# A decoder layer with PEER experts: second search over 96 candidate sums, index gather in fp16

## The chip, the cores and the metric

The kernel runs on one core of a Trainium2 chip. The metric is device time in microseconds, from several timed runs of the same program; beside them there is one profiled execution, from which all the rows below come. The engines are called TensorE (PE; PEld is its weight load), VectorE (DVE), ScalarE (ACT), GpSimd (POOL) and SyncE (SP, which issues the DMAs).

## The reference, cut to what matters

The layer mixes tokens with two attention groups and then runs a PEER block on 256 tokens. Only the PEER block is touched. For each token and each of 8 heads it takes the best 16 of two lists of 128 scores, forms all 256 sums of the two, takes the best 16 sums, and looks up which experts they stand for:

```python
v1, i1 = lax.top_k(s1, P_TOPK)            # P_TOPK = 16, s1 and s2 are (T, 8, 128)
v2, i2 = lax.top_k(s2, P_TOPK)
cand = (v1[..., :, None] + v2[..., None, :]).reshape(T, P_HEADS, P_TOPK * P_TOPK)
vals, ci = lax.top_k(cand, P_TOPK)
e = (jnp.take_along_axis(i1, ci // P_TOPK, axis=-1) * N_KEYS
     + jnp.take_along_axis(i2, ci % P_TOPK, axis=-1))
g = jax.nn.softmax(vals, axis=-1)
...
a = jnp.einsum('cd,ckd->ck', xc, expert_u[ec])
w = (gc * jax.nn.gelu(a.astype(jnp.float32))).astype(x.dtype)
return jnp.einsum('ck,ckd->cd', w, expert_v[ec])
```

Both lists come out in descending order, so a sum of the a-th of one and the b-th of the other (from 0) is beaten or equalled by (a+1)(b+1) - 1 others; only pairs with (a+1)(b+1) up to 16 can be among the best 16.

## The kernel before

The kernel does not gather experts. It computes all 128 x 128 experts densely: for each of 128 rows of `u` a product with the tokens (`xproj`, 24 matmuls, line 1101, output `a`), a GELU, a product with a routing weight per token and expert, and then a product with each row of `v` (line 1456, output `y`). The routing weights are built from the 16 chosen pairs of each head by one-hot matrices (`onehots`, lines 1287 and 1291, fp16) multiplied on TensorE (`route_mm`, line 1299, output `g`), four tokens at a time, 64 groups in all. `route_out` (lines 1312 and 1314) brings a group to its place.

The front part (attention, the query projection with `wq`) ends at some 221 us; then a step of the loop over `u` follows for each j from 0 to 127 (s = 16 + j in the code), and at 636 us the loop over `v` begins. Each 512 KB row is loaded by SyncE five steps ahead into one of three `raw` buffers (`load`, line 754). Three steps ahead it is split into two parts of lower precision (`split`): `hi` by ScalarE (line 769), then `lo` = raw - hi, 1024 columns, by VectorE or by GpSimd (line 772). `xproj` of step j first uses `hi` (16 matmuls), then `lo` (8 matmuls). The load of j+3 waits for `lo` of j, which frees its buffer.

Which engine makes `lo` is decided when `split` is called: GpSimd while `state["single"]` is True, otherwise VectorE. `single` is True during the two searches of `topk_steps`.

The order of all instructions is written out by hand (`manual_schedule`): each engine works through its instructions in the order in which the code emits them. VectorE's side work is a generator, `work_steps`, and each step calls `work_for(share)`, which adds `share` to a credit (at most 4.0) and takes pieces of work as long as the credit is positive. Each piece gives its own price in a `yield`; `yield None` ends the step's turn. In the loop over `u` the share is 3.15, less 1.3 if this step's `lo` is VectorE's.

For each half of the tokens (tt = 0, 1: 128 tokens each) the side work is:

- first search (lines 1212 to 1217): for 16 score lists of 128, find the best 8, their places, strike them out, and find the next 8;
- line 1220: the places converted to fp32; line 1225: the 256 sums of each head, in two instructions of 1024 elements;
- second search (lines 1231 to 1236): the same over 256 sums for each of 8 heads;
- lines 1241 to 1246: the softmax's argument, and the place split into its two indices by a shift and a mask;
- lines 1254, 1257, 1259: for each of the two indices, in two pieces of 64: compare with 0 to 15, multiply with the places found first, sum up over 16 (a gather by one-hot);
- lines 1265 to 1268: the softmax's end; then `topk_out`: transposes on TensorE (line 1274), and copies of the results into `idx` and `gf` (lines 1279 to 1281).

After both halves the routing starts: each piece is one group of `route_out`, `onehots` and `route_mm` and costs 1.95. In steps j=2 and j=4 `sums` puts a few small VectorE operations (lines 1360 to 1365) and a power on GpSimd (line 151) between the searches.

Of the kernel before, what the change touches and what calls it, by code (L numbers as in the profile page):

```python
# [30 lines left out]
C_I16 = 128  # L31
# [55 lines left out]
def body(tc, nc, ap, dbg=None):  # L87
    V, A, T, G, S = nc.vector, nc.scalar, nc.tensor, nc.gpsimd, nc.sync
# [6 lines left out]
    with ExitStack() as ctx:  # L95
# [74 lines left out]
        con = cst.tile([128, C_N], F32, name="con")  # L170
# [569 lines left out]
        raws, parts, pend, on_vector = {}, {}, {}, {}  # L740
# [37 lines left out]
        h = x  # L778
# [393 lines left out]
        cand = tk[:, 0:2048].rearrange("p (h a b) -> p h a b", h=8, a=16)  # L1172
        candf = tk[:, 0:2048].rearrange("p (h n) -> p h n", h=8)
        top = tk[:, 2048:2304].rearrange("p (m k) -> p m k", m=16)
        ixf = tk[:, 2304:2560].rearrange("p (m k) -> p m k", m=16)
        vals = tk[:, 2560:2688].rearrange("p (h k) -> p h k", h=8)
        res = tk[:, 2688:3072].rearrange("p (a m) -> p a m", a=3)
        abf = tk[:, 3072:3328].rearrange("p (a m) -> p a m", a=2)
        ixu = tk[:, 3328:3584].bitcast(U32).rearrange("p (m k) -> p m k", m=16)
        ciu = tk[:, 3584:3712].bitcast(U32).rearrange("p (h k) -> p h k", h=8)  # L1180
        abu = tk[:, 3712:3968].bitcast(U32).rearrange("p (a m) -> p a m", a=2)
        eq = sqq[:, 0:1024]
        rq = cst.tile([128, 16], F32, name="rq")
        iot = misc[:, 48:112].bitcast(F16)

# [19 lines left out]
        def topk_steps(tt):  # L1205
            state["single"] = True
            for m in range(16):
                while m >= state["scores"]:
                    yield None
                v8 = top[:, m, :]  # L1210
                s = sc[:, tt, m, :]
# [7 lines left out]
            state["single"] = False  # L1219
            V.tensor_copy(ixf, ixu)  # L1220
            yield 0.3
            tv = top.rearrange("p (h two) k -> p h two k", two=2)
            for q in range(2):
                hs_ = slice(q * 4, q * 4 + 4)
                V.tensor_tensor(cand[:, hs_], tv[:, hs_, 0, :, None].broadcast_to((128, 4, 16, 16)), tv[:, hs_, 1, None, :].broadcast_to((128, 4, 16, 16)), op=ALU.add)
                yield 1.25
            state["single"] = True
            for h in range(8):
                v8 = vals[:, h, :]
                s = candf[:, h, :]  # L1230
                V.max(out=v8[:, 0:8], in_=s)
                V.max_index(out=ciu[:, h, 0:8], in_max=v8[:, 0:8], in_values=s)  # L1232
                V.match_replace(out=s, in_to_replace=v8[:, 0:8], in_values=s, imm_value=LOWEST)  # L1233
                yield 1.45
                V.max(out=v8[:, 8:16], in_=s)
                V.max_index(out=ciu[:, h, 8:16], in_max=v8[:, 8:16], in_values=s)  # L1236
                yield 0.95
            state["single"] = False

            g = res[:, 2, :].rearrange("p (h k) -> p h k", h=8)  # L1240
            V.tensor_tensor(g, vals, vals[:, :, 0:1].broadcast_to((128, 8, 16)), op=ALU.subtract)
            V.tensor_tensor(g, g, rq[:, tt * 8:(tt + 1) * 8, None].broadcast_to((128, 8, 16)), op=ALU.mult)
            cf = ciu.rearrange("p h k -> p (h k)")
            V.tensor_scalar(abu[:, 0, :], cf, 4, None, op0=ALU.logical_shift_right)
            V.tensor_scalar(abu[:, 1, :], cf, 15, None, op0=ALU.bitwise_and)
            V.tensor_copy(abf, abu)
            yield 1.4
            iv = ixf.rearrange("p (h two) k -> p h two k", two=2)
            i16 = con[:, C_I16:C_I16 + 16]
            for w in range(2):  # L1250
                for q in range(2):
                    e4 = eq.rearrange("p (h k a) -> p h k a", h=4, k=16)
                    e3 = eq.rearrange("p (m a) -> p m a", m=64)
                    V.tensor_tensor(e3, i16[:, None, :].broadcast_to((128, 64, 16)),  # L1254
                                    abf[:, w, q * 64:(q + 1) * 64, None].broadcast_to((128, 64, 16)), op=ALU.is_equal)
                    yield 1.25
                    V.tensor_tensor(e4, e4, iv[:, q * 4:(q + 1) * 4, w, None, :].broadcast_to((128, 4, 16, 16)), op=ALU.mult)
                    yield 1.25
                    V.tensor_reduce(out=res[:, w, q * 64:(q + 1) * 64], in_=e3, axis=AX.X, op=ALU.add)
                    yield 1.25  # L1260
                if w == 0:

                    A.activation(out=g, in_=g, func=AF.Exp)
# [138 lines left out]
        for s in range(NQ, NQ + NU):  # L1402
# [28 lines left out]
                    (G if j < 127 else V).tensor_tensor(dst[:, :, :td], a[:, :, :td], dst[:, :, :td], op=ALU.mult)  # L1431
                state["done"] = j + 1
            td = state["routed"]
            work_for(3.15 - (1.3 if on_vector.get(s + 3) else 0))


        ya = [[bank("y") for n in range(2)] for tt in range(2)]
# [94 lines left out]
```

## Time and profile before

| | |
|---|---|
| median of 3 timed runs | 987.67 us (987.41 to 989.28) |
| profiled execution, its own time | 989.98 us |
| its span, first to last instruction | 988.2 us |
| mean granted TensorE clock | 0.981 of full speed |
| TensorE matmul busy | 949.2 us (96%) |
| VectorE busy | 742.2 us (75%) |
| ScalarE busy | 499.1 us (51%) |
| GpSimd busy | 184.9 us (19%) |

A busy time is the sum of an engine's instructions in the span. A timeline names each instruction with its start, its duration, its engine, line, operation and tiles, and in brackets the idle time before it with what ended it. Durations of neighbours on VectorE overlap by some 0.08 us, so that what an instruction costs in a row of its kind is the distance of the starts.

### The profile page before, as it was taken

The numbers are of one execution on the slowest core, as the hardware profiler recorded it, in microseconds if no ns is written. First come the engines' busy times: TensorE is split into PE (matmuls) and PEld (weight loads), VectorE is DVE, ScalarE is ACT, GpSimd is POOL, SyncE is SP. The second block draws the span as 40 slices with busy tenths as digits, with TensorE's granted clock in tenths as the row PEclk, the third lists the DMA queues.
The fourth block names the chain that finished last, engine by engine and source line by source line (L and its number), as shares of the span: only waits on it lengthen the run. The fifth ranks groups of instructions, "written<-read, shape, count | busy, mean of one in ns | idle before, by whom it ended". The sixth has DMA issues, their size and how long they took to land.

```text
span 988.2 us, 17195 instructions
## 1 busy us (share of the span) xinstructions
PE 949.2 (96%) x6657; PEld 858.0 (87%) x6657; DVE 742.2 (75%) x1379; ACT 499.1 (51%) x920; POOL 184.9 (19%) x148
## 2 busy tenths in 40 slices
PE   7699899999799898999999999999999999999998
PEld 6487678999799898999999999988888888888886
DVE  7576988777989997888999998566666666666664
ACT  4445766655264354555445444455554444455552
POOL 5462524265207500000011112100000000000000
PEclk9799999999799998999999999999999999999999
DMA  7522521654466456455545545565666565665664
GB/s 240 206 91 85 188 66 48 209 171 130 129 205 198 145 157 211 135 166 161 159 151 168 153 152 169 189 194 193 193 193 195 194 195 196 195 193 192 193 192 149
DMA packets 48958, 166.74 MB, mean 169 GB/s; under 512 B 7276, under 2 KB 8300, under 8 KB 48620
## 3 DMA queue, kind: packets, MB, share of 16 engines
q1 hardware_dynamic: 48876, 165.64, 52.9%
q8 instruction: 52, 0.85, 0.3%
q14 instruction: 30, 0.25, 0.1%
HBM read 163.52 MB, written 2.10 MB: 168 GB/s over the span
## 4 chain that ended last, share of the span: by engine, by line
PE 72%; DVE 16%; DMA 4%; issue 3%; POOL 3%; ACT 2%; SPq 1%; DVEq 0%; POOLq 0%; ACTq 0%
PE y L1456 35%; PE a L1101 23%; PE q L1101 5%; PE g L1299 3%; DVE lo L772 2%; DMA win<-win 2%; PE wo L980 1%; DVE B L1254 1%; DMA raw<-u 1%; PE ak L316 1%; PE s L1392 1%; DVE B L1232 1%; DVE B L1233 1%; DVE B L1236 1%; POOL b_rs L151 1%
## 5 line engine op out<-in xcount | busy, mean ns | idle before, releaser
L772 DVE TENSOR_TENSOR lo<-raw,hi 128x1024 fp32r<-128x1024 f32 x237 | 290.3, 1227 | 90.9 <-ACT hi L769 88.8
L769 ACT ACTIVATE hi<-raw 128x1024 fp32r<-128x1024 f32 x266 | 280.1, 1054 | 75.9 <-DMA raw<-u 71.0
L1456 PE MATMUL y<-hi,w 128*128 128x512 f32 x1024 | 274.6, 389 | 0.0
L1101 PE MATMUL a<-xtT,hi 128*128 128x256 f32 x2048 | 269.8, 285 | 0.0
L1101 PEld LDWEIGHTS a<-xtT,hi 128*128 128x128 f32 x2048 | 252.2, 192 | 0.4 <-issue 0.4
L1456 PEld LDWEIGHTS y<-hi,w 128*128 128x128 f32 x1024 | 192.1, 188 | 40.1 <-ACT w L1200 0.3
L1456 PE MATMUL y<-lo,w 128*128 128x512 f32 x512 | 158.2, 389 | 0.0
L1101 PE MATMUL a<-xtT,lo 128*128 128x256 f32 x1024 | 142.6, 283 | 9.0 <-DVE lo L772 8.9
L1200 ACT ACTIVATE w<-B 128x256 fp32r<-128x256 f32 x128 | 53.5, 418 | 171.2 <-PE y L1456 171.0
L1101 PEld LDWEIGHTS a<-xtT,lo 128*128 128x128 f32 x1024 | 130.4, 191 | 9.9 <-DVE lo L772 9.8
L1456 PEld LDWEIGHTS y<-lo,w 128*128 128x128 f32 x512 | 96.1, 188 | 19.9
L1201 DVE TENSOR_TENSOR w<-B,w 128x256 fp32r<-128x256 f32 x128 | 54.4, 426 | 70.1 <-ACT w L1200 70.1
L772 POOL TENSOR_TENSOR lo<-raw,hi 128x1024 fp32r<-128x1024 f32 x29 | 69.2, 2401 | 71.6 <-ACT hi L769 71.5
L1431 POOL TENSOR_TENSOR B<-gl,B 128x512 f32<-128x512 f32 (+33 forms) x36 | 29.5, 821 | 257.6 <-ACT gl L1430 257.6
L1314 ACT ACTIVATE B<-g 128x64 f32<-128x64 f32 (+28 forms) x120 | 23.3, 243 | 75.0 <-DVE B L1312 75.0
L1287 DVE TENSOR_TENSOR oh<-misc,con 128x1024 f16<-128x1024 f16 x64 | 55.8, 872 | 0.0
L1424 ACT ACTIVATE B<-a 128x512 f32<-128x512 f32 (+33 forms) x60 | 28.4, 473 | 51.1 <-PE a L1101 51.0
L1291 DVE TENSOR_TENSOR oh<-oh,gf 128x1024 f16<-128x1024 f16 x64 | 46.1, 720 | 2.2
L1299 PE MATMUL g<-oh 128*128 128x128 f16 x512 | 40.1, 222 | 3.3 <-DVE oh L1291 3.3
L1312 DVE TENSOR_TENSOR B<-g,B 128x8 f32<-128x8 f32 (+32 forms) x71 | 33.4, 477 | 12.7 <-ACT B L1424 12.5
L1101 PE MATMUL q<-xrT,hi 128*128 128x256 f32 x256 | 35.4, 284 | 0.0
L1299 PEld LDWEIGHTS <-oh 128*128 128x128 f16 x512 | 29.2, 98 | 6.4 <-DVE oh L1287 2.8
(309 smaller groups left out, 931.6 us busy)
## 6 DMA issues: line engine op xcount, KB each, us to landing
raw<-u SPq DMA_DIRECT2D x128, 512.0 KB, 3.5
raw<-v SPq DMA_DIRECT2D x128, 512.0 KB, 4.2
raw<-wq SPq DMA_DIRECT2D x16, 512.0 KB, 3.8
win<-win SPq DMA_DIRECT2D x10, 512.0 KB, 9.3
w<-w SPq DMA_DIRECT2D x8, 512.0 KB, 4.6
wo<-wout SPq DMA_DIRECT2D x8, 512.0 KB, 6.0
wsm<-wu SPq DMA_DIRECT2D x1, 1280.0 KB, 7.9
xx<-x SPq DMA_DIRECT2D x4, 256.0 KB, 3.2
```

The source lines that it names most:

```text
L769: A.activation(out=hi, in_=src, func=AF.Copy)
L772: e.tensor_tensor(lo, src, hi.bitcast(F32), op=ALU.subtract)
L1101: T.matmul(out, lhsT=w[:, k, :], rhs=xT[:, k, q, :], start=(n == 0 and k == 0), stop=(n == 2 and k == 7))
L1200: A.activation(out=w[:, 0, :], in_=b, func=AF.Copy)
L1201: V.tensor_tensor(w[:, 1, :], b, w[:, 0, :].bitcast(F32), op=ALU.subtract)
L1287: V.tensor_tensor(o[:, 0:2].rearrange("p a t (i two) -> p (a t) i two", two=2), iot.rearrange("p (i two) -> p i two", two=2)[:, None].broa ...
L1291: V.tensor_tensor(pairs(o[:, 2:4]), pairs(o[:, 1:2]).broadcast_to((128, 2, 4, 64, 2)), gf[:, t4, :, :, None, :].broadcast_to((128, 2, 4, 6 ...
L1299: T.matmul(b[:, i, :], lhsT=o[:, 0, i, :], rhs=o[:, 2 + q, i, :], start=(q == 0), stop=(q == 1))
L1312: V.tensor_tensor(w, bv[:, c0:m, :], w, op=ALU.mult)
L1424: A.activation(out=dst[:, :, td:], in_=bv[:, :, td:], func=AF.Gelu_apprx_tanh)
L1431: (G if j < 127 else V).tensor_tensor(dst[:, :, :td], a[:, :, :td], dst[:, :, :td], op=ALU.mult)
L1456: T.matmul(ya[tt][n], lhsT=wh[:, q, tt * 128:(tt + 1) * 128], rhs=src[:, n * 512:(n + 1) * 512], start=(jj == 0 and p == 0), stop=(jj == 1 ...
```

## The change

The second search runs over 96 sums of each head instead of 256. They are three rectangles: a = 0, 1 with b = 0 to 15 (32 sums), a = 2, 3 with b = 0 to 7 (16 sums), a = 4 to 15 with b = 0 to 3 (48 sums). The place in the 96 is turned back into a and b by shifts, a conversion to fp32 and sums and maxima. The gather of the indices is done for all 8 heads at once, in fp16, with the comparison's operand widened to pairs, and the sum over 16 by adding halves four times. The prices in the yields change with it, and the share of the loop over `u` goes from 3.15 to 2.95.

```diff
-            for q in range(2):
-                hs_ = slice(q * 4, q * 4 + 4)
-                V.tensor_tensor(cand[:, hs_], tv[:, hs_, 0, :, None].broadcast_to((128, 4, 16, 16)), tv[:, hs_, 1, None, :].broadcast_to((128, 4, 16, 16)), op=ALU.add)
-                yield 1.25
+            V.tensor_copy(j16, con[:, C_I16:C_I16 + 16])
+            for a0, na, nb, o in cuts:
+                V.tensor_tensor(candf[:, :, o:o + na * nb].rearrange("p h (a b) -> p h a b", a=na),
+                                tv[:, :, 0, a0:a0 + na, None].broadcast_to((128, 8, na, nb)),
+                                tv[:, :, 1, None, 0:nb].broadcast_to((128, 8, na, nb)), op=ALU.add)
+            yield 1.3
...
-                yield 1.45
+                yield 0.95
...
-                yield 0.95
+                yield 0.6
...
-            V.tensor_scalar(abu[:, 0, :], cf, 4, None, op0=ALU.logical_shift_right)
-            V.tensor_scalar(abu[:, 1, :], cf, 15, None, op0=ALU.bitwise_and)
-            V.tensor_copy(abf, abu)
-            yield 1.4
+            for i in range(3):
+                V.tensor_scalar(cu[:, 1 + i, :], cu[:, 0, :], 4 - i, None, op0=ALU.logical_shift_right)
+            V.tensor_copy(cif, cu)
+            yield 2.0
+            c = cif[:, 0, :]
+            V.scalar_tensor_tensor(cmb[:, 0, :], cif[:, 2, :], -2.0, cif[:, 1, :], op0=ALU.add, op1=ALU.max)
+            V.scalar_tensor_tensor(cmb[:, 1, :], cif[:, 3, :], -8.0, cmb[:, 0, :], op0=ALU.add, op1=ALU.max)
+            a = cmb[:, 1, :]
+            V.tensor_copy(abf[:, 0], a[:, :, None].broadcast_to((128, 128, 2)))
+            for i, k in enumerate((-16.0, -8.0, -4.0)):
+                V.scalar_tensor_tensor(cmb[:, 2 + i, :], a, k, c, op0=ALU.mult, op1=ALU.add)
+            V.scalar_tensor_tensor(cmb[:, 2, :], cmb[:, 3, :], -16.0, cmb[:, 2, :], op0=ALU.add, op1=ALU.max)
+            V.scalar_tensor_tensor(cmb[:, 2, :], cmb[:, 4, :], -32.0, cmb[:, 2, :], op0=ALU.add, op1=ALU.max)
+            V.tensor_copy(abf[:, 1], cmb[:, 2, :, None].broadcast_to((128, 128, 2)))
+            yield 2.5
...
             for w in range(2):
-                for q in range(2):
-                    e4 = eq.rearrange("p (h k a) -> p h k a", h=4, k=16)
-                    e3 = eq.rearrange("p (m a) -> p m a", m=64)
-                    V.tensor_tensor(e3, i16[:, None, :].broadcast_to((128, 64, 16)),
-                                    abf[:, w, q * 64:(q + 1) * 64, None].broadcast_to((128, 64, 16)), op=ALU.is_equal)
-                    yield 1.25
-                    V.tensor_tensor(e4, e4, iv[:, q * 4:(q + 1) * 4, w, None, :].broadcast_to((128, 4, 16, 16)), op=ALU.mult)
-                    yield 1.25
-                    V.tensor_reduce(out=res[:, w, q * 64:(q + 1) * 64], in_=e3, axis=AX.X, op=ALU.add)
-                    yield 1.25
+                V.tensor_tensor(eq.rearrange("p m (a two) -> p m a two", two=2),
+                                j16.rearrange("p (a two) -> p a two", two=2)[:, None].broadcast_to((128, 128, 8, 2)),
+                                abf[:, w, :, None, :].broadcast_to((128, 128, 8, 2)), op=ALU.is_equal)
+                yield 1.3
+                e4 = eq.rearrange("p (h k) a -> p h k a", h=8)
+                V.tensor_tensor(e4, e4, iv[:, :, w, None, :].broadcast_to((128, 8, 16, 16)), op=ALU.mult)
+                yield 1.3
+                for n in (8, 4, 2):
+                    V.tensor_tensor(eq[:, :, 0:n], eq[:, :, 0:n], eq[:, :, n:2 * n], op=ALU.add)
+                V.tensor_tensor(res[:, w, :], eq[:, :, 0], eq[:, :, 1], op=ALU.add)
+                yield 1.7
...
-            work_for(3.15 - (1.3 if on_vector.get(s + 3) else 0))
+            work_for(2.95 - (1.3 if on_vector.get(s + 3) else 0))
```

The tiles `ixf`, `abf`, `j16` and `eq` are fp16 after the change; `ciu` holds the place and its three shifted copies, `cif` the same in fp32.

## Rows read from the trace of the kernel before

**Rows 1.** The page, busy time: us, share of the span, instructions
```profile
PE 949.2 (96%) x6657; PEld 858.0 (87%) x6657; DVE 742.2 (75%) x1379; ACT 499.1 (51%) x920; POOL 184.9 (19%) x148
```

**Rows 2.** Waits of TensorE, 180 to 640 us: total, times, longest
```profile
PE a L1101 <- DVE lo L772: 8.9, 2, 6.3
```

**Rows 3.** Timeline of TensorE: start, duration (us), instruction, idle before and releaser
```profile
250.24 1.07 PE L1101 MATMUL a<-xtT,lo 128*128 128x256 f32 x8
...
264.81 2.08 PE L1101 MATMUL a<-xtT,lo 128*128 128x256 f32 x8 [6.25 <-DVE lo L772]
...
271.40 1.98 PE L1101 MATMUL a<-xtT,hi 128*128 128x256 f32 x16
...
290.69 2.10 PE L1101 MATMUL a<-xtT,hi 128*128 128x256 f32 x16
...
328.04 1.31 PE L1101 MATMUL a<-xtT,lo 128*128 128x256 f32 x8 [2.61 <-DVE lo L772]
...
332.47 1.10 PE L1101 MATMUL a<-xtT,lo 128*128 128x256 f32 x8
...
388.23 1.01 PE L1299 MATMUL g<-oh 128*128 128x128 f16 x8 [3.32 <-DVE oh L1291]
...
394.06 0.62 PE L1299 MATMUL g<-oh 128*128 128x128 f16 x8
...
397.40 0.62 PE L1299 MATMUL g<-oh 128*128 128x128 f16 x8
```

**Rows 4.** Stretch: us, busy by engine, granted clock, DMA share, GB/s
```profile
260.00:275.00 15.00, 10.19 (x64) 10.19 (x65) 14.72 (x24) 4.60 (x6) 0.00 (x0) 0.66 0.44 117
```

**Rows 5.** Timeline of VectorE: first instructions of search rounds, second search, first search
```profile
250.56 0.41 DVE L1231 MAX8 B<-B 128x8 f32<-128x256 f32 x1
...
252.94 0.41 DVE L1231 MAX8 B<-B 128x8 f32<-128x256 f32 x1
...
297.99 0.28 DVE L1212 MAX8 B<-B 128x8 f32<-128x128 f32 x1
...
299.70 0.28 DVE L1212 MAX8 B<-B 128x8 f32<-128x128 f32 x1
```

**Rows 6.** Timeline of VectorE: conversion, decode, gather, copying out
```profile
229.19 0.30 DVE L1220 CAST B<-B 128x256 f32<-128x256 uint32 x1
...
262.43 0.27 DVE L1241 TENSOR_TENSOR B<-B 128x128 f32<-128x128 f32 x1
...
263.54 1.22 DVE L772 TENSOR_TENSOR lo<-raw,hi 128x1024 fp32r<-128x1024 f32 x1
264.68 1.22 DVE L1254 TENSOR_TENSOR B<-con,B 128x1024 f32<-128x1024 f32 x1
...
268.20 1.22 DVE L1259 TENSOR_REDUCE B<-B 128x64 f32<-128x1024 f32 x1
...
296.53 0.75 DVE L1279 CAST con<-rT 128x256 f16<-128x256 f32 x2
```

**Rows 7.** VectorE's groups, 390 to 612 us: busy us, mean ns, idle before
```profile
L1287 DVE TENSOR_TENSOR oh<-misc,con 128x1024 f16<-128x1024 f16 x62 | 54.5, 878 | 0.0
L1291 DVE TENSOR_TENSOR oh<-oh,gf 128x1024 f16<-128x1024 f16 x63 | 45.4, 720 | 2.2
```

**Rows 8.** Timelines of GpSimd and VectorE: operations side by side
```profile
243.48 9.54 POOL L772 TENSOR_TENSOR lo<-raw,hi 128x1024 fp32r<-128x1024 f32 x4
243.54 4.73 DVE L1365 TENSOR_SCALAR rq<-rq,misc 128x8 f32<-128x8 f32 x2 [3.03 <-POOL rq L151]
...
561.12 1.03 POOL L1431 TENSOR_TENSOR B<-gl,B 128x384 f32<-128x384 f32 x1 [5.70 <-ACT gl L1430]
561.30 1.40 DVE L1287 TENSOR_TENSOR oh<-misc,con 128x1024 f16<-128x1024 f16 x1
...
564.98 0.68 DVE L1287 TENSOR_TENSOR oh<-misc,con 128x1024 f16<-128x1024 f16 x1
```

**Rows 9.** Timeline of GpSimd during the first search of half 1
```profile
296.92 14.32 POOL L772 TENSOR_TENSOR lo<-raw,hi 128x1024 fp32r<-128x1024 f32 x6 [43.90 <-ACT hi L769]
```

More of the change, by code (lines that the diff above doesn't have):

```diff
@@ L1171, in body @@
         sc = Bf[:, 96 * 256:112 * 256].rearrange("p (t m n) -> p t m n", t=2, m=16)
-        cand = tk[:, 0:2048].rearrange("p (h a b) -> p h a b", h=8, a=16)
-        candf = tk[:, 0:2048].rearrange("p (h n) -> p h n", h=8)
+        candf = tk[:, 0:768].rearrange("p (h n) -> p h n", h=8)
+        cuts = ((0, 2, 16, 0), (2, 2, 8, 32), (4, 12, 4, 48))
         top = tk[:, 2048:2304].rearrange("p (m k) -> p m k", m=16)
-        ixf = tk[:, 2304:2560].rearrange("p (m k) -> p m k", m=16)
+        ixf = tk[:, 2304:2432].bitcast(F16).rearrange("p (m k) -> p m k", m=16)
         vals = tk[:, 2560:2688].rearrange("p (h k) -> p h k", h=8)
         res = tk[:, 2688:3072].rearrange("p (a m) -> p a m", a=3)
-        abf = tk[:, 3072:3328].rearrange("p (a m) -> p a m", a=2)
+        abf = tk[:, 3072:3328].bitcast(F16).rearrange("p (a m two) -> p a m two", a=2, two=2)
         ixu = tk[:, 3328:3584].bitcast(U32).rearrange("p (m k) -> p m k", m=16)
-        ciu = tk[:, 3584:3712].bitcast(U32).rearrange("p (h k) -> p h k", h=8)
-        abu = tk[:, 3712:3968].bitcast(U32).rearrange("p (a m) -> p a m", a=2)
-        eq = sqq[:, 0:1024]
+        ciu = tk[:, 3584:4096].bitcast(U32).rearrange("p (a h k) -> p a h k", a=4, h=8)
+        cif = tk[:, 768:1280].rearrange("p (a m) -> p a m", a=4)
+        cmb = tk[:, 1280:1920].rearrange("p (a m) -> p a m", a=5)
+        j16 = tk[:, 1920:1928].bitcast(F16)
+        eq = sqq[:, 0:1024].bitcast(F16).rearrange("p (m a) -> p m a", a=16)
         rq = cst.tile([128, 16], F32, name="rq")
@@ L1231, in topk_steps @@
                 V.max(out=v8[:, 0:8], in_=s)
-                V.max_index(out=ciu[:, h, 0:8], in_max=v8[:, 0:8], in_values=s)
+                V.max_index(out=ciu[:, 0, h, 0:8], in_max=v8[:, 0:8], in_values=s)
                 V.match_replace(out=s, in_to_replace=v8[:, 0:8], in_values=s, imm_value=LOWEST)
-                yield 1.45
+                yield 0.95
                 V.max(out=v8[:, 8:16], in_=s)
-                V.max_index(out=ciu[:, h, 8:16], in_max=v8[:, 8:16], in_values=s)
-                yield 0.95
+                V.max_index(out=ciu[:, 0, h, 8:16], in_max=v8[:, 8:16], in_values=s)
+                yield 0.6
             state["single"] = False
@@ L1242, in topk_steps @@
             V.tensor_tensor(g, g, rq[:, tt * 8:(tt + 1) * 8, None].broadcast_to((128, 8, 16)), op=ALU.mult)
-            cf = ciu.rearrange("p h k -> p (h k)")
-            V.tensor_scalar(abu[:, 0, :], cf, 4, None, op0=ALU.logical_shift_right)
-            V.tensor_scalar(abu[:, 1, :], cf, 15, None, op0=ALU.bitwise_and)
-            V.tensor_copy(abf, abu)
-            yield 1.4
+            cu = ciu.rearrange("p a h k -> p a (h k)")
+            for i in range(3):
+                V.tensor_scalar(cu[:, 1 + i, :], cu[:, 0, :], 4 - i, None, op0=ALU.logical_shift_right)
@@ L1248, in topk_steps @@
+            V.scalar_tensor_tensor(cmb[:, 2, :], cmb[:, 3, :], -16.0, cmb[:, 2, :], op0=ALU.add, op1=ALU.max)
+            V.scalar_tensor_tensor(cmb[:, 2, :], cmb[:, 4, :], -32.0, cmb[:, 2, :], op0=ALU.add, op1=ALU.max)
+            V.tensor_copy(abf[:, 1], cmb[:, 2, :, None].broadcast_to((128, 128, 2)))
+            yield 2.5
             iv = ixf.rearrange("p (h two) k -> p h two k", two=2)
-            i16 = con[:, C_I16:C_I16 + 16]
             for w in range(2):
-                for q in range(2):
-                    e4 = eq.rearrange("p (h k a) -> p h k a", h=4, k=16)
-                    e3 = eq.rearrange("p (m a) -> p m a", m=64)
-                    V.tensor_tensor(e3, i16[:, None, :].broadcast_to((128, 64, 16)),
-                                    abf[:, w, q * 64:(q + 1) * 64, None].broadcast_to((128, 64, 16)), op=ALU.is_equal)
-                    yield 1.25
-                    V.tensor_tensor(e4, e4, iv[:, q * 4:(q + 1) * 4, w, None, :].broadcast_to((128, 4, 16, 16)), op=ALU.mult)
-                    yield 1.25
-                    V.tensor_reduce(out=res[:, w, q * 64:(q + 1) * 64], in_=e3, axis=AX.X, op=ALU.add)
-                    yield 1.25
+                V.tensor_tensor(eq.rearrange("p m (a two) -> p m a two", two=2),
[9 more added lines that the diff above has]
+                yield 1.7
```

## Prediction

> **What bounds the kernel now.** I read the page's busy line first: TensorE is busy for 96% of the span, VectorE for 75% [rows 1]. So the change, which only touches VectorE work, can win no more than the time in which TensorE waits for VectorE while that work is under way. The waits of TensorE over that stretch (180 to 640 us) come next: two for a `lo`, 8.9 us together [rows 2], and one for a one-hot, 3.32 [rows 3]. TensorE's timeline around them [rows 3] shows what each costs. A step of the loop over `u` (I name steps by j) is 24 matmuls; seven of them with three transposes lie between the starts of j=14 at 271.40 and j=21 at 290.69, which is 2.72 us for a step. After the first wait 32 matmuls take 271.40 - 264.81 = 6.59 us instead of 3.63; after the second 24 take 332.47 - 328.04 = 4.43 instead of 2.72; after the third a step with its routing takes 394.06 - 388.23 = 5.83 instead of 397.40 - 394.06 = 3.34. So each wait is followed by 3.0, 1.7 and 2.5 us of slow matmuls, and the granted clock shows it: 0.66 on average over 260 to 275 [rows 4], a stretch partly at the lower level, 1.2 instead of 2.4 GHz, after the idle time. Costs: 6.25 + 3.0 = 9.2 at j=12, 2.61 + 1.7 = 4.3 at j=33, 3.32 + 2.5 = 5.8 at j=52: **19.3 us is all that the change can win here**. The rest of the loop, the 64 routing groups included, is TensorE's own work and is the same in both kernels.
>
> **The removed work, by rows.** One round of the first search (128 wide) takes 299.70 - 297.99 = 1.71 us, one of the second (256 wide) 252.94 - 250.56 = 2.38 [rows 5]. The slope is 0.67 per 128 columns, so 96 wide is an estimated 1.71 - 0.17 = 1.54: 8 x 0.84 = 6.7 us less for each half of the tokens (I call them halves 0 and 1). The sums: 2 x 1.14 before, from starts 1.14 apart for 1024 elements (263.54 to 264.68) [rows 6]; after, 768 elements in three pieces, 0.86 plus two more starts of some 0.07, 1.0. Gather before: compare, multiply and reduce of 1024 fp32 elements, each 1.22 busy and 1.14 between starts [rows 6], some 0.1 more where one needs the one before it, four times: 14.1 us. After: fp16 at 1024 elements took 0.68 us undisturbed [rows 8], 0.88 and 0.72 on average [rows 7], so twice the columns is some 1.2; per index 1.2 + 1.2, then halvings of 1024, 512, 256 and 128 elements, 0.69 + 0.4 + 0.3 + 0.3 = 1.7, in all 8.2 for both. Added: the decode. Before it is 263.54 - 262.43 = 1.1 with the two steps on `g` [rows 6]; after, `g` 0.5, three shifts 0.5 and a conversion of 512 elements 0.4 (256 took 0.30 [rows 6]) make 1.5, then seven operations of 128 elements at 0.23 to 0.31 and two widening copies at 0.33 make 2.6. Net saving 6.7 + 1.3 + 5.9 - 3.0 = some 10.9 us of VectorE per half. None of it counts by itself; what counts is when VectorE delivers the three late results.
>
> **What moves.** I counted the code's own yields against the credits of `work_for` (no times in it). Before: half 0's last search round is handed out in step j=8, so the `lo` of j=12 is the first on VectorE behind it; half 1 has `lo` of j=33 and j=34 on VectorE between the two searches, because `single` is False when `split` asks. After: the conversion and the sums cost 0.3 + 1.3 credits and start and end inside one step, so `split` never sees False there. The `lo` of j=4, 5 and (half 1) all to j=34 stay on GpSimd. Half 0's search ends in step j=5, first VectorE `lo` is j=9's; half 1 starts in step j=17 instead of 21, its conversion and sums fall in j=26, its decode in j=31, first VectorE `lo` is j=35's. Routing starts at j=44 instead of 52, but a share of 2.95 - 1.3 = 1.65 against 1.95 for a group lets one step in six or seven pass, and the last group leaves at j=119 in both kernels. No DMA is added; loads follow the `lo` that frees their buffer.
>
> **The new wait: GpSimd.** A VectorE operation of 8 elements took 2.4 us twice (4.73 for two) while GpSimd ran `lo` back to back, 9.54 / 4 = 2.4 us each, and an fp16 two-input operation took 1.40 instead of 0.68 beside a GpSimd product of 1.03 [rows 8]. The searches themselves are not slowed by GpSimd's `lo`. By the Trainium skill, "SBUF — State Buffer", section on the two separate sides, a port pair is shared by both engines and held for a whole instruction, against VectorE operations with two SBUF inputs or in a two-port mode; the rows agree, and the rule speaks against this change, since by it each of the new conversion, copy and sums may wait. Before, the conversion and the sums ran while GpSimd was idle (0.30 for the conversion [rows 6]). After, GpSimd runs one `lo` of 2.39 us (14.32 / 6 [rows 9]) in each 2.72 us step, busy 88%, just there. Behind the waiting operation VectorE's whole second search is queued, behind that the first `lo`, and TensorE waits for that. Price for conversion, copy and three sums: between nothing and one `lo` each for copy and sums, 0.8 + 4 x 2.4 = 10.4. I take 0.8 (rest of one `lo`) for the conversion, 2.4 for the copy and nothing for the sums, since a second operation right behind a waiting one mostly goes through: the mean of the later product, 0.72, against 0.88 of the compare ahead of it [rows 7].
>
> **First wait, after.** VectorE is unchanged up to 229.19 [rows 6]. Conversion 0.2, copy behind j=5's `lo` on GpSimd 2.5, sums 1.0: 232.9. Five rounds: 240.6. The small operations of `sums` 0.8, the power on GpSimd 3.0 (3.03 waited for it) [rows 8]: 244.4. The two small operations behind it wait for one `lo` instead of two, as j=9's is no longer GpSimd's: 246.8. Three rounds 4.6, decode's first part 1.5, `lo` 1.2: 254.1. TensorE wants it at 250.24 [rows 3]. Wait 3.9, slow matmuls 2.2 (they were 1.7 to 3.0): 6.1 in place of 9.2.
>
> **Second wait.** Without the first, j=17 would start at 250.24 - 1.81 + 8 x 2.72 = 270.2; so 276.3. Before, the results of half 0 were copied out 5.8 us behind the step that hands this out (296.53 against 290.69 [rows 3, 6]), VectorE being still behind with `lo`; I take 5: 281.3. Copying out 1.5 (296.53 to 297.99 [rows 5, 6]), 16 rounds 27.4, the port 3.2, conversion, copy, sums 1.4: 314.8. Eight rounds 12.3, decode 1.5 + 2.6, `lo` 1.2: 332.4. TensorE reaches that group of j=35 at 276.3 + 0.25 + 18 x 2.72 + 1.81 = 327.3. Wait 5.1, slow matmuls 2.4: 7.5 in place of 4.3.
>
> **Third wait.** Before, VectorE has 8 x 1.14 of `lo` and 14.1 of gather in eight steps, 23.2 us against 21.8 of TensorE, and comes to the one-hots without any lead. After, it has 5 x 1.14 + 8.2 = 13.9 in five steps of 13.6 and keeps the lead that the slow matmuls give it, about 3 us. So 3.3 - 3 = 0.3, no drop of the clock: 0.3 in place of 5.8.
>
> **Sum.** 6.1 + 7.5 + 0.3 = 13.9 against 19.3: 5.4 us less. The profiled execution took 989.98 us (span 988.2, 1.8 around it), so 984.6 in such a one; it stood 2.3 above the median of the three timed runs, 987.67, which gives **982.3**.
>
> **Rivals.**
> (1) The port does not bite, conversion, copy and sums fitting into GpSimd's gaps: 0.8 to 2.4 sooner in half 0, 3.2 in half 1. Waits 3.1 + 2.0 and 1.9 without a slow stretch, the third between 0.3 and 4 as the lead is smaller: 7.3 to 11 in place of 19.3, or 976 to 979. For it: the conversion before shows no wait. Against: the 2.4 us rows. Chance 0.2.
> (2) Copy and sums wait in turn, 4.8 more at the second wait: 9.9 + 3.0, sum 19.3, **987.7, no change**. For it: the two 8-element operations each lost a whole `lo` [rows 8]. Chance 0.18.
> (3) Slower: multiply and halvings in fp16 run at one element per cycle as fp32 does. Then an index costs some 2.2 + 2.2 + 2.5, 5.6 us more per half; a step has 1.14 of `lo` and about 2.5 of gather against 2.72, and from 1.58 of gather per step on TensorE waits in every step. The two leads of some 3 us are used up, and the third wait returns with 5.5: 982.3 + 2 x 2.6 + 5.5 = 993. Against: both fp16 forms of rows 7, one of them a multiply with a repeated operand. Chance 0.1.
> By the Trainium skill, "VectorE: DVE Perf Modes", the mode 2x_1P needs 16-bit tensors with unit step; all but the last halving are so here, which lowers that chance; without it I would say 0.15.
> (4) VectorE's saving lies beside TensorE's work anyway and the waits come back in other places: within 0.2%, part of (2).
>
> **How the numbers follow.** Forecast (980 to 986) 0.52, (1) 0.2, (2) 0.18, (3) 0.1. The forecast's chain also carries the lag at j=17 (2.4 to 5.8 us behind instead of 5) and TensorE's pace: the same groups took 1.07 or 1.10 us at full clock [rows 3], up to 0.1 per step over some 50 steps, but where VectorE sets the end a slower TensorE only waits less. The range takes in (1) but for its end and (2): 975.5 to 988.5; it leaves out (3) and some of the tails. About 0.2%, 2 us, is what a measurement of this kernel can tell from no change. Faster by more: 0.48 + 0.19 = 0.67; same 0.04 + 0.17 = 0.21; slower 0.12.
>
> **What would show it.** TensorE's waits: one near j=9 of 3 to 5 us, one near j=35 of 4 to 6, none at the first routing. The conversion, copy and sums of half 1 (some 310 to 315 us) with one duration near 2.4. Search rounds 1.5 apart, fp16 compare and multiply near 1.2. Routing from j=44 with a free step after six or seven. Wrong if the waits stand elsewhere, if no VectorE operation is stretched beside GpSimd, or if a wait at each gather step appears.

## The result, and the profile after

The kernel after takes 982.9 us (median of 12 runs, 980.5 to 986.0), the kernel before beside it 987.7 (12 runs). The ratio is 0.9948, with a 95% interval of 0.9936 to 0.9960: 0.5% faster, some 5 us. The forecast was 982.3, with a range of 975.5 to 988.5. The profiled execution took 981.5 us. It lies 8.5 us below that of the kernel before, but 1.5 of them stand ahead of the loop over `u`, which the change does not touch: TensorE's first matmul of that loop starts at 219.56 instead of 221.09.

Busy time, from the page of the kernel after (answers to [rows 1]): VectorE has 18.9 us less work (forecast 2 x 10.9), TensorE's share is the same 96%.

```profile
PE 944.3 (96%) x6657; PEld 853.9 (87%) x6657; DVE 723.3 (74%) x1403; ACT 500.4 (51%) x924; POOL 185.4 (19%) x151
```

Waits of TensorE from 180 to 640 us in the kernel after (total, times, longest; answers to [rows 2]): two waits for `lo` are left, the one for a one-hot is gone.

```profile
PE a L1101 <- DVE lo L772: 8.1, 2, 4.4
```

TensorE's timeline in the kernel after (answers to [rows 3]), around the waits at j=9 and j=35 and at the first routing:

```profile
252.60 2.07 PE L1101 MATMUL a<-xtT,lo 128*128 128x256 f32 x8 [3.73 <-DVE lo L772]
...
259.00 1.98 PE L1101 MATMUL a<-xtT,hi 128*128 128x256 f32 x16
...
331.02 2.08 PE L1101 MATMUL a<-xtT,lo 128*128 128x256 f32 x8 [4.40 <-DVE lo L772]
...
337.47 1.98 PE L1101 MATMUL a<-xtT,hi 128*128 128x256 f32 x16
...
359.61 0.62 PE L1317 MATMUL g<-oh 128*128 128x128 f16 x8
...
362.95 0.62 PE L1317 MATMUL g<-oh 128*128 128x128 f16 x8
```

After each wait 32 matmuls take 259.00 - 252.60 = 6.40 and 337.47 - 331.02 = 6.45 us instead of 3.63, so 2.8 us are lost both times. The granted clock in these stretches (answers to [rows 4]; the last three columns are clock, DMA share, GB/s) is near the lower level, 1.2 instead of 2.4 GHz:

```profile
252.60:259.00 6.40, 6.40 (x33) 6.40 (x33) 6.26 (x13) 1.54 (x2) 0.00 (x0) 0.56 0.58 168
331.00:337.50 6.50, 6.48 (x33) 6.48 (x34) 6.36 (x8) 2.91 (x4) 0.00 (x0) 0.55 0.60 176
```

The sum is 3.73 + 2.77 + 4.40 + 2.82 = 13.7 us in place of 19.3; I had forecast 13.9. VectorE's timeline in the kernel after (answers to [rows 5, 6] and the first part of [rows 8]): the two small operations behind the power, then conversion, copy, sums and the first two rounds of half 1's second search, and the late `lo` of j=35 and 36.

```profile
242.89 2.51 DVE L1383 TENSOR_SCALAR rq<-rq,misc 128x8 f32<-128x8 f32 x2 [3.03 <-POOL rq L151]
...
309.27 1.00 DVE L1224 CAST B<-B 128x256 f16<-128x256 uint32 x1
310.19 0.16 DVE L1226 CAST B<-con 128x16 f16<-128x16 f32 x1
310.27 3.29 DVE L1229 TENSOR_TENSOR B<-B 128x256 f32<-128x256 f32 x3
313.59 0.26 DVE L1237 MAX8 B<-B 128x8 f32<-128x96 f32 x1
...
315.15 0.24 DVE L1237 MAX8 B<-B 128x8 f32<-128x96 f32 x1
...
329.75 2.35 DVE L772 TENSOR_TENSOR lo<-raw,hi 128x1024 fp32r<-128x1024 f32 x2
```

GpSimd beside it (answers to [rows 9]): `lo` after `lo`, 2.7 to 3.0 us apart, and none after 318.4.

```profile
307.72 2.40 POOL L772 TENSOR_TENSOR lo<-raw,hi 128x1024 fp32r<-128x1024 f32 x1 [0.30 <-ACT hi L769]
310.44 2.50 POOL L772 TENSOR_TENSOR lo<-raw,hi 128x1024 fp32r<-128x1024 f32 x1 [0.32 <-ACT hi L769]
313.46 4.92 POOL L772 TENSOR_TENSOR lo<-raw,hi 128x1024 fp32r<-128x1024 f32 x2 [0.52 <-ACT hi L769]
```

VectorE's groups in the kernel after (busy us, mean ns, idle before), gather from 250 to 350 us, then the one-hots from 390 to 612 us (answers to [rows 7]): the fp16 operations of 2048 elements take as long as the fp32 ones of 1024 did [rows 6].

```profile
L1273 DVE TENSOR_TENSOR B<-B 128x2048 f16<-128x2048 f16 x4 | 4.9, 1224 | 0.0
L1268 DVE TENSOR_TENSOR B<-B 128x2048 f16<-128x2048 f16 x4 | 4.9, 1222 | 0.0
...
L1276 DVE TENSOR_TENSOR B<-B 128x1024 f16<-128x1024 f16 x4 | 2.8, 689 | 0.0
...
L1305 DVE TENSOR_TENSOR oh<-misc,con 128x1024 f16<-128x1024 f16 x55 | 51.1, 929 | 0.0
L1309 DVE TENSOR_TENSOR oh<-oh,gf 128x1024 f16<-128x1024 f16 x55 | 39.0, 709 | 1.9
```

So the forecast number held, and so did the places of the waits. The experiments ask whether the reasons did.

### The profile page after: what moved, and what is told of

Its sections match the earlier page's. It is cut to its first block, busy times and chain, and to the rows that moved or that the text cites. A ratio compares the mean times of both kernels' runs of the same rounds, so it can differ in the third digit from the quotient of the medians.

```text
span 979.7 us, 17225 instructions
## 1 busy us (share of the span) xinstructions
PE 944.3 (96%) x6657; PEld 853.9 (87%) x6657; DVE 723.3 (74%) x1403; ACT 500.4 (51%) x924; POOL 185.4 (19%) x151
## 4 chain that ended last, share of the span: by engine, by line
PE 77%; DVE 11%; DMA 5%; POOL 3%; ACT 1%; issue 1%; SPq 1%; DVEq 0%; POOLq 0%; ACTq 0%
PE y L1474 36%; PE a L1101 28%; PE q L1101 4%; PE g L1317 3%; DMA win<-win 3%; PE wo L980 1%; DVE lo L772 1%; DMA raw<-u 1%; PE s L1410 1%; PE ak L316 1%; POOL b_rs L151 1%; DMA B<-keys 1%; DVE B L1217 1%; DVE B L1218 1%; PE oA L697 1%
## 5 line engine op out<-in xcount | busy, mean ns | idle before, releaser
L1449 POOL TENSOR_TENSOR B<-gl,B 128x512 f32<-128x512 f32 (+37 forms) x40 | 32.0, 801 | 273.7 <-ACT gl L1448 273.7
L1332 ACT ACTIVATE B<-g 128x64 f32<-128x64 f32 (+32 forms) x120 | 24.2, 250 | 72.6 <-DVE B L1330 72.6
L1442 ACT ACTIVATE B<-a 128x512 f32<-128x512 f32 (+37 forms) x60 | 27.7, 461 | 62.6 <-PE a L1101 62.6
L1330 DVE TENSOR_TENSOR B<-g,B 128x448 f32<-128x448 f32 (+28 forms) x70 | 32.2, 466 | 18.2 <-ACT B L1442 18.1
L1101 PEld LDWEIGHTS q<-xrT,hi 128*128 128x128 f32 x256 | 32.0, 189 | 0.0
```

What stands on the lines that cost most here:

```text
L1101: T.matmul(out, lhsT=w[:, k, :], rhs=xT[:, k, q, :], start=(n == 0 and k == 0), stop=(n == 2 and k == 7))
L1330: V.tensor_tensor(w, bv[:, c0:m, :], w, op=ALU.mult)
L1442: A.activation(out=dst[:, :, td:], in_=bv[:, :, td:], func=AF.Gelu_apprx_tanh)
```

## The parts of the change, one at a time

**The share alone.** The kernel before with one number changed:

```diff
-            work_for(3.15 - (1.3 if on_vector.get(s + 3) else 0))
+            work_for(2.95 - (1.3 if on_vector.get(s + 3) else 0))
```

> The kernel before with one number changed: the share of the loop over u is 2.95 instead of 3.15; search and gather are those of before. My theory (the third wait went because the gather on VectorE became shorter): nothing of it is shorter here, so the three waits stay, about 6.3 at j=12, 2.6 near j=35 and 3.3 at the first routing, 987.7 within 2 us. Rival (the lower share alone takes the third wait away, because it hands out VectorE's work later and VectorE comes to the one-hots with a lead): the third wait falls to 0 to 1.5 us without slow matmuls behind it, 982 to 985.

Measured: 986.1 us, ratio 1.000 (0.9976 to 1.0024). The time is what my theory said, for another reason: the second wait fell to 1.55 and the third to 2.21 us, with little slow work behind them, but routing starts at j=55 and does not end in the loop. At j=126 the code hands out all that is left, and TensorE's timeline of this kernel shows it waiting there, again with slow matmuls behind:

```profile
622.66 0.62 PE L1299 MATMUL g<-oh 128*128 128x128 f16 x8
625.77 0.62 PE L1299 MATMUL g<-oh 128*128 128x128 f16 x8 [2.50 <-DVE oh L1291]
627.76 0.88 PE L1299 MATMUL g<-oh 128*128 128x128 f16 x8 [1.36 <-DVE oh L1291]
628.39 3.48 PE L1101 MATMUL a<-xtT,hi 128*128 128x256 f32 x16
```

From j=120 to j=127 it takes 28.4 us, the kernel after 19.8. Some 4 of these 8.6 us are eight routing groups (0.5 us of TensorE each) that the kernel after has behind it by then; most of the rest is the two waits, and the slow 3.48 comes on top.

**The share undone.** The kernel after with 3.15 again:

```diff
-            work_for(2.95 - (1.3 if on_vector.get(s + 3) else 0))
+            work_for(3.15 - (1.3 if on_vector.get(s + 3) else 0))
```

> The kernel after with the share put back to 3.15. My theory: the waits at j=9 (3.7) and near j=35 (4.4) stay, and none comes at the routing, since the shorter gather leaves VectorE its lead: within 2 us of the kernel after, 981 to 985. Rival (the share carries the gain): more VectorE work is handed out ahead of each late lo, the second wait splits into several and the third returns with 2 to 3 us: 985 to 989, no gain over before.

Measured: 985.3 us, ratio 0.9997 (0.9978 to 1.0017): no gain that can be told from nothing is left (the kernel before beside it has a median of 987.1), the rival's case. TensorE's timeline of this kernel shows the third wait back, although the gather is the short one; between the waits shown there are three more, of 2.0, 0.45 and 0.40 us.

```profile
253.61 2.08 PE L1101 MATMUL a<-xtT,lo 128*128 128x256 f32 x8 [4.70 <-DVE lo L772]
...
328.48 1.19 PE L1101 MATMUL a<-xtT,lo 128*128 128x256 f32 x8 [0.98 <-DVE lo L772]
...
359.39 0.61 PE L1317 MATMUL g<-oh 128*128 128x128 f16 x8 [3.46 <-DVE oh L1309]
```

**The gather undone.** The kernel after with the gather of before; search and share as after:

```diff
-        ixf = tk[:, 2304:2432].bitcast(F16).rearrange("p (m k) -> p m k", m=16)
+        ixf = tk[:, 2304:2560].rearrange("p (m k) -> p m k", m=16)
...
             for w in range(2):
-                V.tensor_tensor(eq.rearrange("p m (a two) -> p m a two", two=2),
...
+                for q in range(2):
...
+                    V.tensor_tensor(e3, i16[:, None, :].broadcast_to((128, 64, 16)),
+                                    cmb[:, 1 + w, q * 64:(q + 1) * 64, None].broadcast_to((128, 64, 16)), op=ALU.is_equal)
...
```

> The kernel after with the gather of before (fp32, four pieces of compare, multiply and reduce, 14.1 us a half instead of 8.2; the two widening copies go too); the 96-wide search and the share of 2.95 stay. My theory: VectorE has 23 us of work in the eight steps behind the search against 21.8 of TensorE and comes to the one-hots without a lead, so the third wait of 3.3 with 2.5 of slow matmuls returns: 987 to 989. Rival (share and search carry the gain, the gather's saving lies beside TensorE): waits as in after, none at the routing, 981 to 985.

Measured: 979.0 us, ratio 0.9924 (0.9900 to 0.9948), faster than the kernel after and outside both expectations. And again, beside the kernel after on the same chip:

> The kernel with only the gather undone, again, beside the kernel after. If its 4 us under the kernel after came from the gather: 977 to 980 again, 3 to 5 below the kernel after. If it was the run's own variation (its waits with their slow matmuls sum to 13.3 against 14.0 in after): 980 to 983, within 2 us of the kernel after.

> The kernel after as it is, beside the next one on the same chip: 981 to 985, waits of 3.7 and 4.4 as seen.

Measured: 979.5 us, ratio 0.9920 (0.9892 to 0.9949), against 982.6, ratio 0.9953 (0.9938 to 0.9969). The intervals just overlap, so "faster without the fp16 gather" is likely and not certain; that the fp16 gather gains nothing here is certain enough. There is no wait at the routing in either run. In the profiles the loop over `u` is 2.0 and 3.1 us shorter than in the two of the kernel after. Counted as what the steps around them take beyond 2.72 each, the waits cost 13.3 and 12.0 us against 14.0 and 14.1, which makes 0.8 and 2.1 of it. Most of the rest is TensorE's pace: a step without routing takes 2.72 us ahead of the first routing group and 2.83 behind the last one (the two paces are at the end of this document). In the kernel after eight such steps, j=120 to 127, stand behind the last group; with the gather undone the routing runs from j=52 to 126, and eight more stand ahead of the first: 8 x 0.11 = 0.9 us.

**The search undone.** The kernel after with the sums, the 256-wide search and the decode of before, gather in fp16, share 2.95:

```diff
-            for a0, na, nb, o in cuts:
...
+            for q in range(2):
+                hs_ = slice(q * 4, q * 4 + 4)
+                V.tensor_tensor(cand[:, hs_], tv[:, hs_, 0, :, None].broadcast_to((128, 4, 16, 16)), tv[:, hs_, 1, None, :].broadcast_to((128, 4, 16, 16)), op=ALU.add)
...
```

> The kernel after with the sums, the search over 256 and the decode of before; the fp16 gather and the share of 2.95 stay. My theory: the first wait is that of before again (j=12, 6.3 and 3.0 behind it), the second some 2.5 and 1.7, the third 0 to 1: 13.5 to 15 in all, so 982.5 to 984.5, as fast as the kernel after although the search alone is 6.7 us longer per half. Rival (the 96-wide search carries the gain): 986 to 988.

Measured: 984.0 us, ratio 0.9964 (0.9947 to 0.9980), as my theory said, and not to be told from the kernel after. The parts are off, though: 6.39 at j=12, 3.56 for a `lo`, 2.22 at the routing, in a profiled execution that took 987.0 us, 3 above the median.

**What follows.** Neither the lower share nor VectorE's two savings make the gain by themselves. With the share at 3.15 both savings together gain nothing that can be told; at 2.95 there is a gain with either one, and without both the routing runs out of steps. The savings matter as credits that are no longer handed out: they start the routing at j=44 to 52 instead of 55, and this is what allows the lower share.

**Where the third wait came from.** VectorE's timeline of the kernel before, just ahead of the wait at 388.23 [rows 3], shows it idle:

```profile
380.09 1.23 DVE L772 TENSOR_TENSOR lo<-raw,hi 128x1024 fp32r<-128x1024 f32 x1 [1.63 <-ACT hi L769]
383.03 1.23 DVE L772 TENSOR_TENSOR lo<-raw,hi 128x1024 fp32r<-128x1024 f32 x1 [1.72 <-ACT hi L769]
384.17 0.75 DVE L1279 CAST con<-rT 128x256 f16<-128x256 f32 x2
...
386.76 0.69 DVE L1287 TENSOR_TENSOR oh<-misc,con 128x1024 f16<-128x1024 f16 x1
```

And ScalarE's timeline of the same stretch shows what it waited for:

```profile
381.94 1.06 ACT L769 ACTIVATE hi<-raw 128x1024 fp32r<-128x1024 f32 x1 [1.40 <-DMA raw<-u]
```

The copies for the first one-hot stand in VectorE's order behind a `lo` whose load had landed late; each load waits for the `lo` three steps ahead of it. In the kernel with the share undone VectorE idles 1.57 and 2.01 us at the same place. But it idles there in the kernels without this wait too: 1.78 and 0.41 in the kernel after, 1.58 and 1.43 in the second run with the gather undone. So these gaps by themselves do not make the wait.

What goes with the wait is VectorE's lead. In every kernel here TensorE asks for the first one-hot 8.5 to 8.8 us after it starts the transposes of half 1 (`rT`). VectorE first ends the softmax, then makes four or five `lo` at the pace of the loads, then copies. The softmax ends 0.58 us ahead of the transposes in the kernel before and 3.69 in the kernel after. VectorE's and TensorE's timelines with the share undone (0.12) and, below, with the gather undone, first run (3.95):

```profile
346.83 0.29 DVE L1286 TENSOR_TENSOR B<-B,s 128x128 f32<-128x128 f32 x1
...
347.24 0.49 PE L1292 MATMUL rT<-con,B 128*128 128x128 f32 x3
```

```profile
366.75 0.29 DVE L1281 TENSOR_TENSOR B<-B,s 128x128 f32<-128x128 f32 x1
...
370.99 0.49 PE L1287 MATMUL rT<-con,B 128*128 128x128 f32 x3
```

So the length of the gather does not decide by itself. The share has a part in it, by an estimate: a credit of the long gather takes some 0.94 us (14.1 us at prices of 15.0 in all), one of the short gather 0.95 (8.2 at 8.6), and a step gives VectorE a `lo` (1.14) and share - 1.3 credits. That is 2.9 us of work at 3.15, more than a step of 2.72, and 2.7 at 2.95. The slow matmuls behind TensorE's second wait have a part too: where they are missing (two `lo` given to GpSimd, below), the lead is 0.60 even at 2.95. The share alone and the search undone had leads of 3.05 and 2.85, but five `lo` instead of four ahead of the copies, and waits of 2.2. How much each part is worth was not tried apart.

## GpSimd beside VectorE

**Half 0: the wait for the power.** Two small operations on `rq` stand behind GpSimd's power and then beside a `lo`: 3.03 idle and 2.51 in the timeline of after above. The factor is moved into the operation on `g` that needs `rq`:

```diff
-            V.tensor_tensor(g, g, rq[:, tt * 8:(tt + 1) * 8, None].broadcast_to((128, 8, 16)), op=ALU.mult)
+            V.scalar_tensor_tensor(g, g, rs2[:, tt:tt + 1], rq[:, tt * 8:(tt + 1) * 8, None].broadcast_to((128, 8, 16)), op0=ALU.mult, op1=ALU.mult)
...
-            for tt in range(2):
-                V.tensor_scalar(rq[:, tt * 8:tt * 8 + 8], rq[:, tt * 8:tt * 8 + 8], rs2[:, tt:tt + 1], None, op0=ALU.mult)
```

> The kernel after, with VectorE's wait for GpSimd in the middle of half 0's second search taken away: the two small operations on rq behind GpSimd's power (5.45 us from the last small operation ahead of them to their end: 3.03 idle, 2.4 beside a lo) go, and their factor is put into the one operation on g that needs rq. My theory now (the first wait is GpSimd's time in VectorE's queue, not the length of the search): VectorE has the lo of j=9 some 4.5 to 5.4 us earlier, the wait of 3.7 and the 2.9 of slow matmuls behind it go, the second wait stays at 4.4: 975.5 to 977.5. Rival (the saving comes back at the second wait, since VectorE loses the lead that the first wait gave it): second wait of 7 to 8, 979.5 to 982.5.

Measured: 976.7 us, ratio 0.9889 (0.9854 to 0.9924). TensorE's waits in this kernel:

```profile
PE a L1101 <- DVE lo L772: 4.7, 1, 4.7
```

The first wait is gone and did not come back at the second, which is 4.69 instead of 4.40. So the first wait was GpSimd's time in VectorE's queue: taking it out is worth 0.6%, while undoing the search, 6.7 us of VectorE's time a half, could not be told from the kernel after.

**Half 1: two `lo` given to GpSimd**, which is idle from 318.4 us on:

```diff
-                e = G if (s % 2 if s < NQ else s < NQ + NU and state["single"]) else V
+                e = G if (s % 2 if s < NQ else s < NQ + NU and state["single"] or s - NQ in (35, 36)) else V
...
-            on_vector[s] = s >= 6 and e is V
+            on_vector[s] = s >= 6 and (e is V or s - NQ in (35, 36))
```

> The kernel after, with only the lo of j=35 and j=36 made by GpSimd instead of VectorE; the credits, and so the order of all else, stay as they are. GpSimd is idle from 318.4 us on, while TensorE waits until 331.0 for the lo of j=35. Theory (the second wait is VectorE's queue, and GpSimd could have made these two in time): no wait at j=35 and j=36, one of 1 to 1.5 at j=37 without slow matmuls: 976 to 978.5. Rival (GpSimd's lo then stand beside the decode's operations with two inputs, each of which loses up to 2.4): a wait of 3.5 to 6 at j=37, 981 to 984.

Measured: 978.6 us, ratio 0.9918 (0.9890 to 0.9946), just above the theory's 978.5. TensorE's timeline of this kernel has a short wait at j=37 with the full pace behind it, as expected, and one at the routing, which I had not expected (VectorE's lead there is 0.60):

```profile
333.68 1.20 PE L1101 MATMUL a<-xtT,lo 128*128 128x256 f32 x8 [1.07 <-DVE lo L772]
...
356.43 0.61 PE L1317 MATMUL g<-oh 128*128 128x128 f16 x8 [1.77 <-DVE oh L1309]
```

**Doubling the suspected cost: the sums head by head**, from one execution:

```diff
-            for a0, na, nb, o in cuts:
-                V.tensor_tensor(candf[:, :, o:o + na * nb].rearrange("p h (a b) -> p h a b", a=na),
...
             for h in range(8):
+                for a0, na, nb, o in cuts:
+                    V.tensor_tensor(candf[:, h, o:o + na * nb].rearrange("p (a b) -> p a b", a=na),
...
```

> The kernel after, with the sums made for one head at a time, three small operations ahead of each of the eight rounds of the second search instead of three large ones ahead of all. It doubles the suspected cost: how often VectorE comes to a two-input operation beside GpSimd. Theory (each time it waits for GpSimd's lo to end, up to 2.4): while GpSimd is busy a round goes from 1.54 to some 2.7, three or four rounds in each half; the first lo of each half comes 3 to 4 us later, waits of 6.5 to 7.5 and 8 to 8.5, no wait at the routing, 989 to 991. Rival (the waits of 2.3 seen in after come from the sums' own strided operands): only the small operations' own time, some 0.35 a head, 1.8 a half: 985 to 987.

Measured: 990.2 us, in the expected span, but the theory has only half of it. In half 0, VectorE's timeline of this kernel shows one group of three operations that takes 4.61 instead of 0.38 us, nearly two `lo` of GpSimd:

```profile
234.31 4.61 DVE L1232 TENSOR_TENSOR B<-B 128x32 f32<-128x32 f32 x3
...
240.51 0.38 DVE L1232 TENSOR_TENSOR B<-B 128x32 f32<-128x32 f32 x3
```

That made the power late, and behind the power in GpSimd's order stood the `lo` of j=8. GpSimd's timeline of this kernel shows it idle 6.66 us until VectorE delivered, and TensorE waited 4.33 us for GpSimd, a wait that no other kernel here has:

```profile
245.41 2.91 POOL L151 TENSOR_TENSOR rq<-rs_x,mhalf 128x16 f32<-128x16 f32 x1 [6.66 <-DVE rs_x L150]
```

In half 1 only two of the eight groups were stretched (0.92 and 1.17 us instead of 0.38), not three or four, since GpSimd had run out of `lo`. There the small operations' own time, some 2.4 us more, was the larger part, as the rival had it; the conversion ahead of them lost 2.2 us as well.

**The price changes from one execution to the next.** Undisturbed, the conversion takes 0.29, the copy 0.16 and the three sums 1.08 us. In half 1 of the kernel after their excess was 0.7 + 0 + 2.2, in its second profile 0.3 + 2.2 + 0; with the gather undone 0.8 + 4.4 and 1.0 + 2.2 (there is no copy); with the search undone 2.0 + 2.2 + 0. That is one to two `lo`. With the share undone it was only 0.4 in all, in the two paced kernels below with the 96-wide search 1.3 and 0: there GpSimd stood idle around the sums, waiting for a `hi`. VectorE's timelines with the gather undone, first run, and with the search undone:

```profile
317.17 1.09 DVE L1222 CAST B<-B 128x256 f32<-128x256 uint32 x1
318.19 5.49 DVE L1226 TENSOR_TENSOR B<-B 128x256 f32<-128x256 f32 x3
```

```profile
314.96 2.26 DVE L1223 CAST B<-B 128x256 f16<-128x256 uint32 x1
317.14 2.37 DVE L1225 CAST B<-con 128x16 f16<-128x16 f32 x1
319.43 2.35 DVE L1229 TENSOR_TENSOR B<-B 128x1024 f32<-128x1024 f32 x2
```

So my rival of waiting in turn does happen, in one execution and not in another of the same program: with the gather undone the second wait of TensorE was 6.71 and 3.54 us, and of the difference the port makes 2.0 (5.2 against 3.2); in the second run the matmuls behind the first wait were also 1.4 us slower, which brings TensorE later to the second. By the Trainium skill, "SBUF — State Buffer", section on the two separate sides, whichever of the two engines starts first has the port pair for its whole instruction. The trace agrees: with the search undone the 0.29 us conversion takes 2.26, up to 317.2, where the first of two `lo` begun at 314.67 (4.81 for both) ends. How many turns VectorE lost in a row was 0 to 2 here.

## A kernel whose TensorE doesn't wait

If what counts is when `lo` goes back to VectorE, then the code should hand out a search no faster than VectorE does it, so that GpSimd makes `lo` until VectorE has caught up. Together with the folded factor of the half 0 experiment:

```diff
-            work_for(2.95 - (1.3 if on_vector.get(s + 3) else 0))
+            work_for((2.35 if state["single"] else 3.05) - (1.3 if on_vector.get(s + 3) else 0))
```

With the fp32 gather and the 96-wide search:

> The kernel with the gather undone (fp32, 96-wide search), the two operations behind the power taken away as above, and the share 2.35 while a search is under way, 3.05 otherwise. Theory (what counts is that the code hands VectorE its search no faster than VectorE does it, so that lo stays with GpSimd until VectorE has caught up; the gather's length lies beside TensorE): no wait of TensorE over 1 us from 225 to 640 us, 966 to 971. Rival (the 14.1 us of fp32 gather then have no cover and the third wait returns): a wait of 2 to 4 at the first routing with slow matmuls behind it, 971 to 976.

Measured: 968.9 us, ratio 0.9803 (0.9771 to 0.9836), with no wait of TensorE from 225 us to the end of the loop over `u` (one of 1.2 us for ScalarE follows at the start of the loop over `v`).

With the whole change, fp16 gather included:

> The paced kernel (two operations behind the power gone, share 2.35 in a search and 3.05 otherwise) with the fp16 gather of the change instead of fp32. Theory (5.9 us less of VectorE work a half lies beside TensorE's work): no wait of TensorE in the loop, the same as the kernel paced with the fp32 gather, 967 to 971. Rival (the fp16 gather costs something of its own, as the kernel with the gather undone came out 4 us under the kernel after): 971 to 974.

Measured: 970.2 us, ratio 0.9821 (0.9796 to 0.9846), no wait either.

With nothing of the change, the kernel before with these two edits (2.35 and 3.15):

> The kernel before, with nothing of the change, but with the two operations behind the power taken away and the share 2.35 in a search and 3.15 otherwise. Theory (what sets the time is when lo goes back to VectorE, and both searches have cover as long as GpSimd makes lo): no wait over 1 us at lo, 968 to 972, below the kernel after although VectorE has some 19 us more work. Rival (256-wide searches push the routing so late that it does not end by j=126 and the last groups run without cover, 1.2 us each): 973 to 979.

Measured: 967.8 us, ratio 0.9798 (0.9776 to 0.9821). One stretch, 220 to 360 us (busy time of PE, PEld, DVE, ACT, POOL; clock, DMA share, GB/s), of the kernel before and of this one, in this order:

```profile
220.00:360.00 140.00, 131.14 (x1107) 129.90 (x1106) 125.43 (x352) 64.52 (x77) 56.10 (x24) 0.95 0.53 161
```

```profile
220.00:360.00 140.00, 140.00 (x1242) 139.21 (x1241) 127.95 (x341) 76.52 (x89) 75.86 (x33) 1.00 0.61 189
```

TensorE is busy throughout at a granted clock of 1.00, and GpSimd makes 31 `lo` there instead of 22. VectorE is busy for 733 us in this kernel's span and for 717 in the paced one with the whole change: 16 us of its work are worth no time. The three are within each other's intervals. All three beat the kernels before and after. How the gain divides between the two edits was tried apart only on the kernel after (the fold alone: 982.9 to 976.7).

## Why the prediction was right, and where its steps failed

- **The bound** (only TensorE's waits for VectorE count, 19.3 us at most) held: the paced kernels are 17 to 20 us under the kernel before, up to the bound as far as these runs can tell, and have no such wait left.
- **First wait**: forecast 3.9 and 2.2 of slow matmuls at j=9, measured 3.73 and 2.77. The step through GpSimd (one `lo` instead of two for the small operations) was read rightly. What I did not see is that it was most of the wait: without it there is none.
- **Second wait**: forecast 5.1 and 2.4 at j=35, measured 4.40 and 2.82. The lag behind j=17 was 280.36 - 275.57 = 4.8 (forecast 5), the port's price 2.9 (forecast 3.2). I had put it on the conversion and the copy; the copy fell into a gap of GpSimd and the sums waited (3.29 instead of 1.08; in half 0 likewise, 3.27), in the next profile it was the copy. That the price came out near the forecast is partly luck: the same kinds of operations lost from nothing to 5.2 us in the other kernels.
- **Third wait**: forecast 0.3, measured none. That VectorE's lead counts was read rightly (forecast about 3 us, measured 3.69 at the transposes). **The step that failed** is what takes the lead away: I had put it on the length of the gather alone, and given the share no part. With the long gather and the share of 2.95 the lead is 3.95 and there is no wait; with the short one and 3.15 it is 0.12, and the wait is 3.46. So this number was right for a reason that the runs do not bear out.
- **The share** stood in the prediction as something that lets a step in six or seven pass. The gain hangs on it: without it the ratio is 0.9997, with it alone 1.000.
- **VectorE's rows**: a round of the 96-wide search 1.56 us between the starts at 313.59 and 315.15 (forecast 1.54); fp16 compare and multiply 1.22 each (forecast 1.2). The decode's first part, whose terms sum to 1.4 and not to the 1.5 written, took 1.4, its second 2.3 (forecast 2.6). The compare and the multiply rule out rival (3). Rival (1) is out by the stretched sums of this kernel, though with the share undone the operations of half 1 fitted into GpSimd's gaps but for 0.4 us. Rival (2), waiting in turn, appeared in other executions but not in this one. Rival (4), VectorE's saving lying beside TensorE, is right for the gather, and I had given it no price of its own.

## What to carry to other kernels

Where one engine is busy for 96%, look for what the others stand behind when it waits (a queue position, a port, a late load) before making their work shorter: in the paced kernels 16 us less of VectorE work were worth nothing, while two operations moved out of GpSimd's way were worth 6 us in the kernel after. Where a hand-written order hands out work by prices, check the price per step against the measured time of a step, and test a part of a change by undoing it alone; the gain may hang on the number that came along (the share).

## What the runs showed of the hardware that was not expected

- TensorE's clock did not always fall after a wait of the same length. TensorE's timeline with the gather undone, first run, has a wait of 3.66 with nearly the full pace and a granted clock of 1.00 behind it, where the kernel after lost 2.8 us behind 3.73 at 0.56 (and the same program as here, run again, 1.7 behind 3.65 at 0.68):

```profile
251.47 1.19 PE L1101 MATMUL a<-xtT,lo 128*128 128x256 f32 x8 [3.66 <-DVE lo L772]
252.50 1.98 PE L1101 MATMUL a<-xtT,hi 128*128 128x256 f32 x16
```

- At a granted clock of 1.00, TensorE has a second, slightly slower pace. These are TensorE's timelines of the kernel after, ahead of the first routing group and behind the last, and of the kernel paced with the fp32 gather, ahead of its first:

```profile
300.17 1.98 PE L1101 MATMUL a<-xtT,hi 128*128 128x256 f32 x16
...
613.39 2.05 PE L1101 MATMUL a<-xtT,hi 128*128 128x256 f32 x16
```

```profile
303.62 2.05 PE L1101 MATMUL a<-xtT,hi 128*128 128x256 f32 x16
```

The slower one makes a step 2.83 instead of 2.72 us. The paced fp32 kernel had it in its profile for 31 steps ahead of the routing, j=23 to 53, some 3.3 us, which is most of what that execution (972.8) lay above the median of 968.9. The kernels before and after run at it from j=120 to 127, behind their last routing group. Nothing in the rows explains it.
